# The mixing layer of a decoder trunk in seven products instead of eight, with its sums made by transfers

## The chip, the cores and the metric

The kernel runs on one core of one Trainium2 chip. Its time is device microseconds of one execution: three runs of the kernel before gave 1323.67, 1324.64 and 1323.67 us, median 1323.67. A profile is one further execution; the times of instructions below are from it, counted from the start of its span.

A core has five engines with a queue each: TensorE (PE in the profile, its weight loads PEld), VectorE (DVE), ScalarE (ACT), GpSimd (POOL) and SyncE (SP), which here only issues transfers. TensorE reads SBUF and writes PSUM, which holds eight banks of 128 x 512 floats.

## The reference, cut to what matters

One decoder layer on 1024 tokens of width 1024, in float32. The change lies in the line that makes `x`, and in what hands it on:

```python
merged = jax.nn.sigmoid(g_da) * (y_da @ w_br_da[l]) + jax.nn.sigmoid(g_sw) * (y_sw @ w_br_sw[l])
x = x + merged @ w_mix_out[l]                      # 1024x1024 times 1024x1024
xn = rmsnorm(x, norm_ffn_w[l])
x = x + conv_ffn(xn, w_up[l], conv_w[l], conv_b[l], w_down[l])
```

## The kernel before, in words

Everything lies transposed, channels on the 128 partitions, tokens along the row; "half" is 512 of the 1024 tokens. A float32 product is made of three matmuls: an operand is cut into a high part (ScalarE rounds it, float32r) and a low part (VectorE subtracts), and high x high, high x low and low x high add up in PSUM (`mm3`, L153; `product`, L895). So every weight that is loaded (`load_w`, L132) costs a transfer from SyncE's queue (L129), a ScalarE cast (L139) and a VectorE subtraction (L141), and every operand the same pair (`split`, L820).

The stages, in order of time:

- `project` (L260): the input projections. Most go in pairs through seven products instead of eight (Strassen's scheme in Winograd's form): `sum_pair` (L94) makes four sums of weights on GpSimd, `split_pair` cuts them, `recombine` (L451) puts the seven results together on VectorE.
- `attention` (L492).
- `rest` (L765): for each of eight output chunks m the two branch products, times the gates (GpSimd L791, ScalarE L798, VectorE L802 and L807), summed on GpSimd (L808; the last on VectorE) and cut into high and low parts mh and ml (L811, L812).
- `mix` (L825): the mixing layer. Eight output chunks, each with eight inner chunks x 2 halves x 3 matmuls into two banks. VectorE adds the result to x (L850), ScalarE's queue stores it and scales it, ScalarE squares (L855, L862), GpSimd adds up the squares in `rstd` (L863). After every second chunk `operands` (L874) makes the operands of the next seven products on VectorE.
- `hidden` (L906): the up projection in seven products for each of 22 pairs, then convolution and gate. For j = 0 it first runs three of four inner chunks of five products, then the fourth, then the column sums of squares (L168), which the norm needs. Its weight sums are on GpSimd (L104 to L107). Beside it `sums_of` (L82) makes the weight sums of `down` in DRAM: plain copies on SyncE's queue (L86) and adding transfers on GpSimd's (L87).
- `down` (L1086): the down projection in seven stages, each a product of one weight block and one operand block, added into x.

Order: the program's order gives priorities, and a compile-time scheduler lays each engine's instructions out by them and by when it reckons them ready; on the chip each engine runs its list in order. `next_w` (L65) loads one weight ahead. Raw weights have three buffers (`raw`), high and low parts two each (`wh`, `wl`), so a cast must wait until TensorE is through with the weight two before.

Of the kernel before, what the change touches and what calls it, by code (L numbers as in the profile page):

```python
# [10 lines left out]
F32 = mybir.dt.float32  # L11
F32R = mybir.dt.float32r
AF = mybir.ActivationFunctionType
ALU = mybir.AluOpType
# [30 lines left out]
class Trunk:  # L45
# [18 lines left out]

    def next_w(self, n=2):  # L65

        self.ahead(n)
        return self.wq.pop(0)
# [13 lines left out]
    def sums_of(self):  # L82

        nc, d = self.nc, self.sd
        row = lambda m, r: self.w_dn[m].rearrange("p k c -> p (k c)")[:, r * HK * P:(r + 1) * HK * P]
# [100 lines left out]
    def run(self):  # L186
        nc, tc = self.nc, self.tc
        with ExitStack() as ctx:
# [23 lines left out]
            self.yd = self.dp.tile([8, P, T], F32, name="yd")  # L212
            self.sd = {n: self.dp.tile([4, P, HK * P], F32, name="sd" + n) for n in ("P5", "P6", "P3", "P7")}
            self.wp = ctx.enter_context(tc.tile_pool(name="wp", bufs=2))
            self.qd = self.dp.tile([18, 2, P, T], F32, name="qd")
            self.xctx = ExitStack()
            self.xp = self.xctx.enter_context(tc.tile_pool(name="xp", bufs=1, side="right", reuse_waits="tile"))
# [11 lines left out]
    def plan(self):  # L229
# [16 lines left out]
        self.mix_order = [m for k in range(4) for m in (k, k + 4)]  # L246
        src += [(self.w_mix[m], KC) for m in self.mix_order]
# [12 lines left out]
    def project(self):  # L260
# [4 lines left out]
        self.xl = [self.xp.tile([P, T], F32R, name=f"xl{k}") for k in range(KC)]  # L265
        self.xact = lambda kc, hf: (self.xh[kc][:, hf * H2:(hf + 1) * H2], self.xl[kc][:, hf * H2:(hf + 1) * H2])
        with ExitStack() as ctx:
# [158 lines left out]
            for m in self.plain[3:]:  # L426
# [27 lines left out]
    def recombine(self, ps, us, tp, o, after=None):  # L454
# [11 lines left out]
        with self.tc.issue_after(after) if after is not None else nullcontext():  # L466
            tt(c12, ps["P3"], u4, ALU.add)  # L467
            tt(c21, u3, ps["P4"], ALU.subtract)
# [295 lines left out]
    def rest(self, gctx):  # L764
        nc, tc = self.nc, self.tc  # L765
        with ExitStack() as ctx:
            e = ctx.enter_context
            mctx = ExitStack()
            mh, ml = [], []
            with gctx, ExitStack() as bctx:  # L770
# [13 lines left out]
                mp = mctx.enter_context(tc.tile_pool(name="mp", bufs=1, side="right", reuse_waits="tile"))  # L784
                for m in range(KC):
# [16 lines left out]
                    nc.vector.tensor_tensor(gs[0], gs[0], ps, ALU.mult)  # L802
                    for hf in range(2):
                        ps = self.tl(self.psG, [P, H2], "g")
                        self.mm3(ps, w, yact[1], hf, range(4), o=4)
                        g = gs[1][:, hf * H2:(hf + 1) * H2]
                        nc.vector.tensor_tensor(g, g, ps, ALU.mult)  # L807
                    (nc.vector if m == KC - 1 else nc.gpsimd).tensor_tensor(gs[0], gs[0], gs[1], ALU.add)  # L808
                    a = mp.tile([P, T], F32R, name=f"mh{m}")
                    b = mp.tile([P, T], F32R, name=f"ml{m}")  # L810
                    nc.scalar.copy(a, gs[0])  # L811
# [500 lines left out]
```

## Time and profile before

| what | value |
|---|---|
| median of three runs | 1323.67 us |
| the profiled execution, its own time | 1325.13 us |
| its span in the profile | 1323.3 us |
| mean granted TensorE clock | 0.997 |
| `rest`'s eight chunks on TensorE | about 500.4 to 587.4 us |
| mixing layer on TensorE | 587.4 to 674.5 us |
| `hidden`, first pair until the column sums | 674.5 to 688.1 us |

1.8 us of the execution's time lie outside the span. A row of a timeline has start, length, engine, line, operation, written tile <- read tiles, and in brackets the idle time before it and what ended it. Lengths of neighbours on one engine overlap: the distance between two starts is what an instruction costs in a row, its length what it costs alone.

### The profile page before, as it was taken

To read this page: it belongs to the slowest core of one execution; us is meant where nothing else is said; L and a number is where in the kernel's file an instruction comes from. 1 tells how busy PE (TensorE), PEld (TensorE's weight loads), DVE (VectorE), ACT (ScalarE), POOL (GpSimd) and SP (SyncE) were. 2 spreads that over 40 slices of the span, in tenths; PEclk is the share of its full clock that TensorE was granted. 3 is DMA by queue.
4 is the path that set the end of the run, shared out by engine and by line. 5 is a ranking of instruction groups with operands and counts; after the bars stand their busy time and mean duration, and the time that the engine had idled before them with its cause. 6 is when DMAs were issued, how large, how long until landed. Compare 5 with 4: busy or idle time off the path is not lost.

```text
span 1323.3 us, 17121 instructions
## 1 busy us (share of the span) xinstructions
PE 1310.0 (99%) x6210; PEld 1089.0 (82%) x6210; DVE 1059.7 (80%) x1456; ACT 621.7 (47%) x967; POOL 480.4 (36%) x364
## 2 busy tenths in 40 slices
PE   9999999999999999999999999999999999999997
PEld 7888888888888878888888888888888888878886
DVE  8846775289888976555668999999999999896855
ACT  9432232276667765333444434333343435554543
POOL 0446652000111015651425667666666742000002
PEclk9999999999999999999999999999999999999998
DMA  7334433976554236334333435564536227953434
GB/s 261 126 143 157 145 146 127 266 184 191 143 128 138 84 127 216 139 111 159 128 111 119 177 134 144 147 210 124 167 138 170 77 86 264 323 192 117 161 98 147
DMA packets 71588, 205.96 MB, mean 156 GB/s; under 512 B 8016, under 2 KB 15824, under 8 KB 71376
## 3 DMA queue, kind: packets, MB, share of 16 engines
q1 hardware_dynamic: 57472, 176.03, 39.2%
q0 software_dynamic: 2304, 11.54, 4.6%
q10 hardware_dynamic: 11728, 17.31, 3.6%
q8 instruction: 49, 0.80, 0.2%
q14 instruction: 35, 0.29, 0.1%
HBM read 156.08 MB, written 71.83 MB: 172 GB/s over the span
## 4 chain that ended last, share of the span: by engine, by line
PE 76%; DVE 11%; issue 5%; DMA 4%; POOL 2%; ACT 1%; SPq 0%; POOLq 0%; DVEq 0%; ACTq 0%
PE t L902 27%; PE y L1125 8%; PE d L1125 4%; PE g L160 4%; PE g L161 4%; PE g L162 4%; PE sc L161 3%; PE sc L160 3%; PE sc L162 3%; PE sc L634 3%; DVE c L1071 2%; DVE wl L120 2%; DVE c L1072 2%; PE t L650 1%; DMA rv<-in_w_up 1%
## 5 line engine op out<-in xcount | busy, mean ns | idle before, releaser
L141 DVE TENSOR_TENSOR wl<-raw,wh 128x1024 fp32r<-128x1024 f32 (+2 forms) x85 | 99.7, 1174 | 53.9 <-ACT wh L139 44.0
L139 ACT CAST wh<-raw 128x1024 fp32r<-128x1024 f32 (+2 forms) x85 | 74.1, 873 | 105.8 <-PE y L1125 43.2
L1055 POOL TENSOR_TENSOR us<-us,rstd 128x1024 f32<-128x1024 f32 x42 | 94.8, 2290 | 48.0 <-DVE us L467 31.5
L1069 ACT ACTIVATE c<-us,vecs 128x1024 f32<-128x1024 f32 x44 | 54.8, 1248 | 118.5 <-POOL us L1055 112.9
L120 DVE TENSOR_TENSOR sl<-sf,sh 128x1024 fp32r<-128x1024 f32 x62 | 94.9, 1532 | 14.7 <-ACT sh L118 14.7
L118 ACT CAST sh<-sf 128x1024 fp32r<-128x1024 f32 x62 | 64.7, 1045 | 83.5 <-PE t L902 44.1
L177 POOL TENSOR_TENSOR rs<-ms,mhalf 128x8 f32<-128x8 f32 (+2 forms) x9 | 13.3, 1473 | 234.6 <-DVE ms L175 228.4
L104 POOL TENSOR_TENSOR sf<-rv 128x512 f32<-128x512 f32 x30 | 54.6, 1819 | 116.6 <-DMA rv<-in_w_up 56.4
L1125 PE MATMUL y<-h,wh 128*128 128x512 f32 (+1 forms) x324 | 95.1, 377 | 0.0
L1125 PE MATMUL d<-h,wh 128*128 128x512 f32 x264 | 81.2, 389 | 0.0
L1072 DVE SCALAR_TENSOR_TENSOR c<-us,vecs,c 128x1024 f32<-128x1024 f32 x44 | 75.4, 1746 | 0.1
L160 PE MATMUL g<-xh,wh 128*128 128x512 f32 x176 | 71.0, 403 | 1.5 <-ACT g L563 1.5
L161 PE MATMUL g<-xl,wh 128*128 128x512 f32 x176 | 70.3, 399 | 0.0
L162 PE MATMUL g<-xh,wl 128*128 128x512 f32 x176 | 70.3, 399 | 0.0
L1125 PEld LDWEIGHTS y<-h,wh 128*128 128x128 f32 x324 | 59.4, 188 | 11.0
L106 POOL TENSOR_TENSOR sf<-raw,rv 128x512 f32<-128x512 f32 x30 | 54.9, 1830 | 36.8 <-DVE sl L120 36.8
L1071 DVE SCALAR_TENSOR_TENSOR c<-us,vecs,c 128x1024 f32<-128x1024 f32 x44 | 64.3, 1490 | 1.8 <-ACT c L1069 1.7
L120 DVE TENSOR_TENSOR wl<-raw,wh 128x1024 fp32r<-128x1024 f32 (+1 forms) x32 | 62.8, 1963 | 0.1
L638 DVE CUSTOM_DVE_ANT_0 L<-sc,bias 128x128 f32<-128x128 f32 (+7 forms) x64 | 47.7, 752 | 17.0 <-PE sc L634 13.7
L617 POOL MEMSET aT<- 128x128 f32 x32 | 6.1, 204 | 151.8 <-PE t L663 98.0
L1125 PE MATMUL y<-h,wl 128*128 128x512 f32 (+1 forms) x162 | 61.1, 377 | 0.0
L639 ACT ACTIVATE L<-L,sm 128x128 f32<-128x128 f32 (+7 forms) x64 | 49.6, 778 | 20.0 <-DVE sm L638 17.3
(394 smaller groups left out, 4160.0 us busy)
## 6 DMA issues: line engine op xcount, KB each, us to landing
u<-qd SPq DMA_DIRECT2D x72, 256.0 KB, 6.1
raw<-in_w_up SPq DMA_DIRECT2D x23, 512.0 KB, 4.7
raw<-in_w_in SPq DMA_DIRECT2D x22, 512.0 KB, 3.8
hd<-c SPq DMA_DIRECT2D x22, 512.0 KB, 2.6
sdP<-in_w_down POOLq DMA_DIRECT2D x16, 704.0 KB, 8.3
rv<-in_w_up SPq DMA_DIRECT2D x21, 512.0 KB, 4.6
hc<-hd SPq DMA_DIRECT2D x33, 256.0 KB, 5.4
gr<-gd SPq DMA_DIRECT2D x16, 512.0 KB, 3.4
```

The costliest lines, as they stand in the source:

```text
L118: cast = nc.scalar.copy(hi, src)
L120: low = nc.vector.tensor_tensor(lo, src, hi.bitcast(F32), ALU.subtract)
L139: self.hi = nc.scalar.copy(wh, raw)
L141: self.lo = (eng or nc.vector).tensor_tensor(wl, raw, wh.bitcast(F32), ALU.subtract)
L160: nc.tensor.matmul(ps, wh[:, kc + o, :], ah, start=first and n == 0, stop=False)
L161: nc.tensor.matmul(ps, wh[:, kc + o, :], al, start=False, stop=False)
L162: nc.tensor.matmul(ps, wl[:, kc + o, :], ah, start=False, stop=last and n == len(kcs) - 1)
L902: nc.tensor.matmul(ps, (ah, ah, al)[p][:, k, :], (bh, bl, bh)[p], start=first and n == p == 0, stop=last and p == 2 and n == len(ks) - 1, ...
L1055: i = (nc.vector if m % NF == 0 else nc.gpsimd).tensor_tensor(us[:, 2:], us[:, 2:], self.rstd, ALU.mult)
L1071: nc.vector.scalar_tensor_tensor(c, us[:, 1:T + 1], cw[1], c, ALU.mult, ALU.add)
L1072: nc.vector.scalar_tensor_tensor(c, us[:, 0:T], cw[0], c, ALU.mult, ALU.add)
L1125: nc.tensor.matmul(ps, v[:, k - k0, :], x, start=start and k == i == 0, stop=k == HK - 1 and i == 2, skip_group_check=True)
```

## The change

The mixing layer too goes in seven products: with merged in four blocks (channel halves by token halves) and the weights in four, P1 = A11 B11, P2 = A12 B21, P5 = S1 T1, P6 = S2 T2, P3 = S4 B22, P7 = S3 T3, P4 = A22 T4, where S are sums of weight blocks and T sums of blocks of merged. A stage is one of these: four output chunks x four inner chunks x three matmuls, in two half stages of one weight load each. Every stage is added into x on VectorE as soon as a chunk is done; P6 and P3, P7 and P4 go on in the banks of the stage before them, so that a bank is added in at the points of its running sum.

- The weight sums S are made in DRAM (`sums_of`, now with arguments) while `project` runs its nine pairs: four steps for each pair, 16 copies on SyncE's queue and 16 adding transfers on GpSimd's, 256 KB each.
- The sums T come from 16 adding transfers within SBUF on GpSimd's queue (`add_on`), 256 KB each: four in `rest`, eight after P1, four after P2. For that the gates write some quarters with a minus sign, and merged stays whole (`mr`). Each T is cut when a stage's buffers are free (`split_m`).
- Weights are loaded 14 times instead of 8, all of 512 KB; results are added to x in 28 pieces of 512 columns instead of 8 of 1024.
- Stores of x, squares and the operands for `hidden` go by chunk and half as these become final: in P2 (four), P3, P7 and P4. `finish` and `onward` hold what `mix` and `operands` held.
- `hidden` begins with P1, P5, P3, P7, then P2, whole, then the column sums; the cut of its operands T2 and T4 moves from there into the mixing layer.
- Memory: eight buffers (`slot`) hold in turn the low parts of the input, operands of the mixing layer, of `hidden` and of `down`; x is loaded into eight buffers in the memory of `rest`.

The core of the diff (removed lines of `mix` and `operands` left out, they stand above):

```diff
+    def slot(self, n, shape=[P, 2, H2], dt=F32R):
+        return self.tl(self.ar, shape, f"x{n}", dt)
...
+            sums = self.sums_of(self.md, self.w_mix, H2)
             for j, ms in enumerate(self.pairs):
                 w = self.next_w()
+                for _ in range(4):
+                    with tc.issue_after(self.sync), tc.issue_after(self.sum):
+                        next(sums, None)
...
+                    def gate(g, ps, hf):
+                        if hf == (m < 4):
+                            nc.vector.scalar_tensor_tensor(g, g, -1.0, ps, ALU.mult, ALU.mult)
+                        else:
+                            nc.vector.tensor_tensor(g, g, ps, ALU.mult)
...
+                    (nc.vector if m == KC - 1 else nc.gpsimd).tensor_tensor(mr[:, m], gs[0], gs[1], ALU.add)
+                    for name, hf in ((("B11", 0),) if m < 4 else (("B21", 0), ("B22", 1))):
+                        k = m % 4
+                        t = M[name, k] if name == "B22" else self.slot(m)
+                        M[name, k] = self.split(t[:, 0], t[:, 1], mr[:, m, hf * H2:(hf + 1) * H2])
+                    if m > 3:
+                        self.add_on(mr, m - 4, 0, m - 4, 1)
...
+    def add_on(self, mr, a, ah, b, bh):
+
+        x, y = (mr[:, c, h * H2:(h + 1) * H2] for c, h in ((a, ah), (b, bh)))
+        self.nc.gpsimd.dma_start(x, y, accum_op=ALU.add)
...
+        def finish(m, hf):
+            x = col(m, hf)
+            nc.scalar.dma_start(self.x2d[m, :, hf * H2:(hf + 1) * H2], x)
+            a = acc[:, hf * H2:(hf + 1) * H2]
+            if m == 0:
+                nc.scalar.activation(a, x, AF.Square)
+            else:
+                sq = sqs[:, len(nsq) % 2]
+                nsq.append(m)
+                nc.scalar.activation(sq, x, AF.Square)
+                nc.gpsimd.tensor_tensor(a, a, sq, ALU.add)
+
+        def onward(m, hf):
+            x, k = col(m, hf), m % 4
+            t = t2[k // 2][:, k % 2]
+            if m < 4:
+                nc.scalar.mul(x, x, wcol(m))
+                if hf == 0:
+                    self.B["B11", k] = parts(up["B11", k], x)
+                else:
+                    tt(t, x, col(k, 0), ALU.subtract)
+                    self.B["T1", k] = parts(up["T1", k], t)
+            elif hf:
+                self.B["B22", k] = parts(up["B22", k], x, wcol(m))
+                u = col(k, 1)
+                stt(u, x, wcol(m), u, ALU.mult, ALU.subtract)
+                tt(t, u, col(k, 0), ALU.add)
+                self.B["T3", k] = parts(self.slot(k), u)
+                self.B["T2", k] = parts(up["T2", k], t)
+            else:
+                u = col(m, 1)
+                stt(u, x, wcol(m), t, ALU.mult, ALU.subtract)
+                self.B["T4", k] = parts(up["T4", k], u)
+                self.B["B21", k] = parts(self.slot(4 + k), x, wcol(m))
...
+                for h in range(2):
+                    w = self.next_w()
+                    if n == 0:
+                        for m in (2 * h, 2 * h + 1, 2 * h + 4, 2 * h + 5):
+                            nc.sync.dma_start(xm[m], self.xT[m])
+                    if stage == "P3" and h:
+                        i = [e[1] for e in self.wsrc].index("pair")
+                        pair = self.sum_pair(self.wsrc.pop(i)[0], True)
+                    for m in (2 * h, 2 * h + 1):
+                        ps = chains[which][m]
+                        for k in range(4):
+                            hi, lo = M[b, k]
+                            for i, (v, x) in enumerate(((w[0], hi), (w[0], lo), (w[1], hi))):
+                                nc.tensor.matmul(ps, v[:, m % 2 * 4 + k, :], x, start=start and k == i == 0, stop=k == 3 and i == 2, skip_group_check=True)
+                        x = col(m + o, hf)
+                        tt(x, x, ps, ALU.subtract if o or stage == "P2" else ALU.add)
+                        if done:
+                            finish(m + o, hf)
+                            late.append((m + o, hf))
+                        while len(late) > (m < 3 and o == 0):
+                            onward(*late.pop(0))
+                if stage == "P1":
+                    split_m("T1", 0, 0)
+                    for k in range(4):
+                        self.add_on(mr, k, 1, k + 4, 1)
+                    for k in range(4):
+                        self.add_on(mr, k, 0, k + 4, 1)
+                elif stage == "P2":
+                    split_m("T2", 4, 0, -1.0)
+                    for k in range(4):
+                        self.add_on(mr, k, 0, k + 4, 0)
+                elif stage == "P5":
+                    split_m("T3", 0, 1)
+                elif stage == "P6":
+                    split_m("T4", 4, 0)
...
+        with tc.high_priority(100):
+            return self.split_pair(*pair)
```

More of the change, by code (lines that the diff above doesn't have):

```diff
@@ new lines, in mix @@
+        xm = {m: xmp.tile([P, T], F32, name=f"xm{m}") for m in (4, 5, 6, 7, 3)}
+        x2ctx = ExitStack()
+        xmp2 = x2ctx.enter_context(tc.tile_pool(name="xmp2", bufs=1, reuse_waits="tile"))
+        xm.update((m, xmp2.tile([P, T], F32, name=f"xm{m}")) for m in (2, 1, 0))
+        sqs = self.tl(self.sfp[0], [P, 2, H2], "t42", bufs=1)
+        t2 = [self.tl(self.cpl, [P, 2, H2], "c") for _ in range(2)]
+        acc, nsq, late = self.rstd, [], []
+        col = lambda m, hf: xm[m][:, hf * H2:(hf + 1) * H2]
```

167 lines of the change are left out of this document (74 added, 93 removed).

## The prediction, as put on record

> **What bounds the kernel now.** I read the page's busy shares first, then one line of the chain that ended last, then the groups of TensorE and the busy times by stage.
>
> ```profile
> PE 1310.0 (99%) x6210; PEld 1089.0 (82%) x6210; DVE 1059.7 (80%) x1456; ACT 621.7 (47%) x967; POOL 480.4 (36%) x364
> 64.07 171.36 PE t L902 x756
> L160 PE MATMUL sc<-mh,wh 128*128 128x512 f32 x128 | 49.8, 389 | 0.0
> L161 PE MATMUL sc<-ml,wh 128*128 128x512 f32 x128 | 49.8, 389 | 0.0
> L162 PE MATMUL sc<-mh,wl 128*128 128x512 f32 x128 | 49.8, 389 | 0.0
> ```
>
> TensorE is busy 99% of the span, so only fewer or shorter matmuls, or fewer gaps, make the kernel faster. The length in a group (389 ns) isn't the price of a matmul, for they overlap: 756 of them in a row take 171.36 us, 0.2267 us each. The mixing layer's 3 x 128 = 384 then take 87.0 us.
>
> ```profile
> core 0: us, PE busy (x) PEld busy (x) DVE busy (x) ACT busy (x) POOL busy (x), PEclk, DMA share, GB/s
> 64.00:235.00 171.00, 171.00 (x756) 141.61 (x755) 112.14 (x116) 49.62 (x59) 84.46 (x50) 1.00 0.39 147
> 587.40:674.70 87.30, 87.30 (x386) 72.18 (x385) 52.11 (x47) 33.94 (x44) 24.96 (x17) 1.00 0.40 138
> 674.70:701.80 27.10, 27.10 (x133) 22.82 (x132) 21.16 (x21) 14.32 (x18) 12.36 (x11) 1.00 0.21 81
> 701.80:1106.00 404.20, 404.00 (x1778) 332.71 (x1777) 397.18 (x348) 163.51 (x179) 250.72 (x177) 1.00 0.46 144
> ```
>
> The third row is the mixing layer: TensorE without a gap, VectorE busy for 52 of 87 us. The last row is `hidden`: TensorE full again, VectorE full beside it (397 of 404). So time that TensorE saves in the mixing layer counts to the end only if VectorE, too, comes to `hidden` that much earlier; a backlog there would stay.
>
> **What goes.** Seven stages of 4 x 4 x 3 = 48 matmuls are 336 instead of 384. 48 x 0.2267 = **10.9 us** less on the engine that sets the end. A stage takes 10.9 us, a half stage with its one weight load 5.44.
>
> **What is added where cover is wide.** In `project` the sums in DRAM add 16 copies on SyncE's queue and 16 issues on GpSimd's.
>
> ```profile
> L87 POOL DMA_DIRECT2D sdP<-in_w_down x16: 795/1058/1150, 800.4 to 1012.7; - x16
> DMA to landing us min/median/max: 2.6/5.2/14.5
> raw<-in_w_mix SPq DMA_DIRECT2D x8, 512.0 KB, 3.9
> ```
>
> An issue of the same kind takes GpSimd 1.06 us, 17 us in all; with them it is busy for 101 of 171 us there. An adding transfer waits at the head of GpSimd's queue for its copy, which was issued a pair earlier (84 matmuls, 19 us) and lands in 14.5 us at worst; behind it stand the next pair's four weight sums, for which there is the rest of that pair. I cost it at nothing; if the cover failed, TensorE would wait for a pair's weights, some us at once. The 16 transfers within SBUF are no row of this trace. By the landing of the nearest ones (2.6 to 14.5 us, for 704 KB against 256) the sums stand long before use: T1's are issued in `rest` and used two stages later, T3's and T2's after P1 and used in P7 and P6, 22 us later or more, T4's after P2 for P4. Nothing, then; the upper end is a chain of three landings of 14.5 us against the 22, some 20 us, which I hold for unlikely. Six more weight loads are 3 MB on transfers that are busy for 0.40 of the time: nothing, as long as the casts keep up (below). The eight loads of x now wait for the memory of `rest`'s last gates, free at about 594.7, and land 3.9 us later or more. The first additions into x wait for them, behind these VectorE's next weight part; TensorE needs P1's banks again only in P6, so the list's order decides: 0 to 2 us, taken as 0 because the scheduler can put the weight part first.
>
> **Where a wait is added: P1's second half.** Until now the weight after the first had 10.9 us; now it has 5.44, until 587.4 + 5.44 = 592.8.
>
> ```profile
> 589.84 1.23 DVE L812 TENSOR_TENSOR ml<-gr,mh 128x1024 fp32r<-128x1024 f32 x1 [3.37 <-ACT mh L811]
> 590.98 1.21 DVE L802 TENSOR_TENSOR gr<-gr,sc 128x1024 f32<-128x1024 f32 x1
> 592.11 1.28 DVE L807 TENSOR_TENSOR gr<-gr,g 128x512 f32<-128x512 f32 x2
> 593.43 1.23 DVE L808 TENSOR_TENSOR gr<-gr,gr 128x1024 f32<-128x1024 f32 x1
> 594.57 1.22 DVE L141 TENSOR_TENSOR wl<-raw,wh 128x1024 fp32r<-128x1024 f32 x1
> 595.77 1.22 DVE L812 TENSOR_TENSOR ml<-gr,mh 128x1024 fp32r<-128x1024 f32 x1
> ```
>
> The weight's low part (L141) is done at 595.8, behind the last chunk's gates. Its first reader is the third matmul of the half, at 593.3. As the row stands, TensorE waits 2.5 us. If the compiler puts the part ahead of the sum at 593.43, as it puts it ahead of L812 here, 1.1 us less. I take **+1.4**, bounds 0 and 2.5.
>
> **Where VectorE becomes full: P3, P7, P4.** Prices in a row: an instruction of 512 columns 0.60 us (L807: two in 1.28, one 0.68), a weight part 1.14.
>
> ```profile
> 598.52 1.22 DVE L850 TENSOR_TENSOR x<-x,sc 128x1024 f32<-128x1024 f32 x1 [1.52 <-PE sc L162]
> 599.66 1.22 DVE L141 TENSOR_TENSOR wl<-raw,wh 128x1024 fp32r<-128x1024 f32 x1
> ```
>
> From the start of P3 until the last part of B21:
> - the cut of T4, left from P6: 4 x 0.60 = 2.4
> - P3: two weight parts 2.3, four additions 2.4, T1 of `hidden` (difference and low part, four times) 4.8: 9.5
> - P7: 2.3 + 2.4, and five instructions for each of four chunks (B22, u, t, T3, T2) 12.0: 16.7
> - P4: one weight part 1.1, four additions 2.4, three for each chunk (u, T4, B21) 7.2, and the first pair's four weight parts, which stand early by their priority, 3 x 1.14 + 0.60 = 4.0: 14.7
>
> Together 43.3 us. TensorE, unhindered, asks for the last B21 only in the fifth product of `hidden`: three stages, four products of 2.72 us and nine matmuls later, 32.7 + 10.9 + 2.0 = 45.6. Alone, VectorE would keep up with 2.3 to spare. But it isn't alone.
>
> ```profile
> 612.43 1.29 POOL L863 TENSOR_TENSOR rstd<-rstd,t 128x512 f32<-128x512 f32 x1 [23.70 <-ACT t L862]
> 614.94 1.68 POOL L863 TENSOR_TENSOR rstd<-rstd,t 128x512 f32<-128x512 f32 x1 [1.22 <-ACT t L862]
> 615.40 1.78 DVE L892 TENSOR_TENSOR c<-c,xw 128x512 f32<-128x512 f32 x1
> 603.15 0.69 DVE L888 TENSOR_TENSOR xw<-xw 128x512 f32<-128x512 f32 x1
> L807 DVE TENSOR_TENSOR gr<-gr,g x16: 672/681/689, 510.8 to 592.7; 128x512 f32<-128x512 f32 x16
> 904.59 2.47 DVE L1071 SCALAR_TENSOR_TENSOR c<-us,vecs,c 128x1024 f32<-128x1024 f32 x2
> 906.68 1.53 POOL L104 TENSOR_TENSOR sf<-rv 128x512 f32<-128x512 f32 x1 [3.09 <-DMA rv<-in_w_up]
> 906.98 4.54 DVE L1072 SCALAR_TENSOR_TENSOR c<-us,vecs,c 128x1024 f32<-128x1024 f32 x2
> 908.28 2.16 POOL L105 TENSOR_TENSOR sf<-sf,raw 128x512 f32<-128x512 f32 x1
> 912.74 2.21 POOL L106 TENSOR_TENSOR sf<-raw,rv 128x512 f32<-128x512 f32 x1 [2.26 <-DVE sl L120]
> 914.91 1.30 POOL L107 TENSOR_TENSOR sf<-raw,sf 128x512 f32<-128x512 f32 x1
> ```
>
> L892 takes 1.78 instead of 0.69: it starts inside GpSimd's L863 and ends just after it. L807, which reads PSUM, never takes over 0.69. So of instructions that read two tensors in SBUF, VectorE's wait for GpSimd's, and the other way round. In the stretch above GpSimd has the pair's four sums and ten of the squares (three in P3, four in P7, three of P4's four): 14 x 1.29 = 18.1 us. How much of it falls on VectorE? Bounds: nothing, if it all lies beside additions that read PSUM or waits for TensorE, and the whole 18.1. The nearest rows are the same four sums in `hidden`, where VectorE is full too: they are 4 x 1.29 = 5.2 us, and VectorE lost 2.1 by them (L1072 twice in 4.54, L1071 twice in 2.47), a share of 0.40. 18.1 x 0.40 = 7.3, less the spare 2.3: TensorE waits **5.0 us**. The other end of the range is 18.1 - 2.3 = 15.8.
>
> **The sum:** -10.9 + 1.4 + 5.0 = **-4.5 us**. The profiled execution took 1325.13 us, 1.8 us more than its span; the next would take 1320.6. The median of the runs shown is 1.46 us under it, so the forecast is 1323.67 - 4.5 = **1319.2**. After the column sums the order is as before (two products, two of the next pair), with VectorE less loaded: the cut of T2 and T4 no longer stands there.
>
> **The rivals.**
>
> *VectorE and GpSimd shut each other out for the whole time; slower.* Then VectorE's stretch is 43.3 + 18.1, TensorE waits 15.8, and -10.9 + 1.4 + 15.8 = +6.3, 1330.0 us. It decides from the point where the 18.1 cost more than 11.8 (10.9 - 1.4 + 2.3), a share of 0.65. For it: the lists are fixed at compile time and the chunks' instructions depend on ScalarE's casts in between, so VectorE also has small waits that my 0.60 leaves out. Against it: 0.40 in `hidden`, where the load is as dense. [...] 0.28.
>
> *The cover holds.* GpSimd's work lies beside additions and waits: -10.9 + 1.4 = -9.5, 1314.2 us. For it: L863 and the sums were no hindrance in the mixing layer before, with VectorE at 52 of 87 us. 0.22.
>
> *The weights of P7 and P4 come late.* From P3's second half on, the pair's raw weights hold two of the three buffers, so each load waits for the one before it.
>
> ```profile
> 589.71 1.05 ACT L139 CAST wh<-raw 128x1024 fp32r<-128x1024 f32 x1
> ```
>
> Transfer 3.9, cast 1.05 and low part 1.22 make 6.2 us against a half stage of 5.44, and where VectorE first finishes a chunk (five instructions, 3.0 us), 9.2: 3.7 late, for each of the last two loads 7.5 in all, in place of the 5.0. -10.9 + 1.4 + 7.5 = -2.0, 1321.7 us, no difference that can be told. 0.17.
>
> That the change doesn't do what it says can't be excluded where a scheduler orders the lists: were the sums by transfer late, P6 or P4 would wait with every engine idle. I count it into the first rival.
>
> **How the numbers follow.** The forecast has 0.33. A measurement of this kernel can tell about 0.2%, 2.6 us, from no change. Forecast and cover are faster: 0.55. The late weights lie within: 0.17. The first rival is slower: 0.28. The range goes from the cover without the wait in P1's second half, 1323.67 - 10.9 = 1312.8, to the first rival, 1330.0; outside are shares over the whole lock and late sums. Forecast and cover alone lie between 1312.8 and 1321.
>
> **What would show it.** The mixing layer has 336 matmuls at 0.2267 us. TensorE has a gap of 1 to 2.5 us about 5.4 us after its first, for L141's row. VectorE is nearly without idle time from P3's end until B21, with lengths over 1 us where GpSimd runs, and TensorE's gaps in P4 and the first products of `hidden` sum to some 5 us, waiting for VectorE. The column sums start at about 684 instead of 688.1, and `hidden` runs as long as before. Wrong would be: gaps of 10 us or more there, waits for an adding transfer, or a longer `project` or `hidden`.

## The result, and the profile after

The changed kernel takes 1342.55 us (median of four runs, 1340.74 to 1345.11) against 1323.85 for the kernel before on the same chip: a ratio of 1.0141, 95% interval 1.0121 to 1.0162. It is slower, and outside the range of the prediction (1312.8 to 1330.0). The profiled execution took 1340.74, 15.6 us more than that of before. The experiments ran on other chips of the same kind, where the kernel before took 1325.5 to 1327.2. They are given as ratios to it. The 2 or 3 us between chips are as large as some effects; so beside each ratio stands **T**, from the first matmul of the mixing layer to the first of the column sums in that run's profile. It was 688.1 - 587.4 = 100.7 us before and is 704.35 - 587.66 = 116.7 after; without any hole it would be 89.8 (336 + 60 matmuls of 0.2267). T comes from one execution, whose time lay up to 3.7 us from the median of its runs, so small differences of T say little. One of e10's ten executions took 1865.92 us, at a mean granted clock of 0.65; its ratio leaves it out.

The busy line of the page after, and the busy times by stage. A row has its stretch and length, then TensorE's time, its weight loads', VectorE's, ScalarE's and GpSimd's, each with the count of instructions, then the granted clock, the share of the transfer engines and GB/s:

```profile
PE 1306.0 (98%) x6162; PEld 1084.2 (81%) x6162; DVE 1087.8 (81%) x1518; ACT 634.4 (47%) x1002; POOL 510.3 (38%) x396
```

```profile
core 0: us, PE busy (x) PEld busy (x) DVE busy (x) ACT busy (x) POOL busy (x), PEclk, DMA share, GB/s
64.00:235.00 171.00, 171.00 (x756) 141.57 (x756) 110.98 (x116) 49.44 (x59) 97.56 (x66) 1.00 0.62 190
587.66:609.50 21.84, 21.84 (x97) 17.83 (x95) 13.64 (x18) 7.83 (x11) 5.65 (x6) 1.00 0.89 271
609.50:628.46 18.96, 13.11 (x49) 9.56 (x48) 12.30 (x16) 11.90 (x19) 6.64 (x6) 0.91 0.76 200
628.46:661.74 33.28, 32.52 (x144) 26.57 (x142) 28.35 (x33) 17.28 (x27) 13.25 (x8) 1.00 0.41 136
661.74:690.74 29.00, 17.40 (x53) 12.48 (x52) 28.88 (x35) 16.61 (x26) 11.64 (x6) 0.71 0.41 136
690.74:717.80 27.06, 27.06 (x133) 22.77 (x132) 14.71 (x18) 8.42 (x12) 12.71 (x11) 1.00 0.17 59
717.80:1122.00 404.20, 402.75 (x1775) 332.09 (x1774) 396.25 (x347) 163.13 (x178) 251.42 (x177) 1.00 0.46 143
```

Three rows are as before: `project` takes in 32 more transfers and is full, the first pair of `hidden` is full, and so is the rest. The whole difference lies in the mixing layer, which now lasts from 587.66 to 690.74, 103.1 us, where 336 matmuls of 0.2267 make 76.2. The second row, P1 and P2, has no gap. The third, P5, loses about 8 us, the fourth (P6, P3, most of P7) under 1, the fifth, the last of P7 and P4, about 17, and there the granted clock is 0.71.

TensorE's groups of the mixing layer (count, busy time, mean ns, idle time before) and the rows of its timeline that stand at the holes:

```profile
L953 PE MATMUL m<-x,wh 128*128 128x512 f32 x192 | 63.6, 418 | 15.1 <-ACT wh L142 15.1
L953 PE MATMUL m<-x,wl 128*128 128x512 f32 x96 | 39.4, 418 | 3.1 <-DVE wl L144 3.1
```

```profile
612.99 0.84 PE L953 MATMUL m<-x,wh 128*128 128x512 f32 x2 [3.41 <-ACT wh L142]
...
615.69 0.63 PE L953 MATMUL m<-x,wl 128*128 128x512 f32 x1
616.12 0.98 PE L953 MATMUL m<-x,wh 128*128 128x512 f32 x2
...
617.64 0.39 PE L953 MATMUL m<-x,wl 128*128 128x512 f32 x1
617.86 0.63 PE L953 MATMUL m<-x,wh 128*128 128x512 f32 x2
...
621.81 1.70 PE L953 MATMUL m<-x,wh 128*128 128x512 f32 x6 [1.04 <-ACT wh L142]
```

```profile
667.72 2.07 PE L953 MATMUL m<-x,wh 128*128 128x512 f32 x4 [5.14 <-ACT wh L142]
...
680.79 2.08 PE L953 MATMUL m<-x,wh 128*128 128x512 f32 x4 [5.47 <-ACT wh L142]
683.85 0.79 PE L953 MATMUL m<-x,wl 128*128 128x512 f32 x1 [0.99 <-DVE wl L144]
```

TensorE waits for the high part of a weight in P5 and ahead of both halves of P4, 18.2 us in all with the low parts. That isn't the 26.9 that are lost. The other 8.7 are matmuls behind the holes: from 615.69 to 616.12 one takes 0.43 us, from 617.64 to 617.86 again 0.22. At half speed go some 4 us behind the first two holes, and 8 behind the last.

Why is the weight late in P5? ScalarE's list, and the transfers between 588 and 620 us (by queue: packets, MB, share; by issue: count, KB, us to landing):

```profile
605.27 0.63 ACT L897 ACTIVATE t<-xm 128x512 f32<-128x512 f32 x1 [0.37 <-DVE xm L955]
611.28 0.72 ACT L904 ACTIVATE xm<-xm,vecs 128x512 f32<-128x512 f32 x1 [5.38 <-DMA x2d<-xm]
611.91 1.03 ACT L142 CAST wh<-raw 128x1024 fp32r<-128x1024 f32 x1
```

```profile
q1 hardware_dynamic: 2096, 5.77, 51.1%
q0 software_dynamic: 866, 1.57, 26.7%
...
raw<-mdP SPq DMA_DIRECT2D x4, 512.0 KB, 13.4
mr<-mr POOLq DMA_DIRECT2D x6, 256.0 KB, 7.6
x2d<-xm ACTq DMA_DIRECT2D x4, 256.0 KB, 5.2
```

`onward` scales a chunk of x in place (L904). So it must wait until the store of that chunk (L890, issued just before) has read it, 5.38 us, and the cast of P5's weight stands behind it in ScalarE's list. By the trace that weight had landed at 608.7, before TensorE was through with P2 (609.4): it was the cast that came late, at 611.91. In the kernel before the scaled x went into another tile (`xw`).

Why is it late in P4? ScalarE's, VectorE's and GpSimd's rows, and the busy times from 646 us on:

```profile
666.10 0.62 ACT L881 CAST x<-xm 128x512 fp32r<-128x512 f32 x1 [2.02 <-DVE xm L913]
666.62 1.04 ACT L142 CAST wh<-raw 128x1024 fp32r<-128x1024 f32 x1
...
676.76 1.99 ACT L121 CAST sh<-sf 128x1024 fp32r<-128x1024 f32 x2 [1.61 <-DVE x L882]
...
679.70 1.04 ACT L142 CAST wh<-raw 128x1024 fp32r<-128x1024 f32 x1
```

```profile
651.48 1.78 DVE L882 TENSOR_TENSOR T<-c,T 128x512 fp32r<-128x512 f32 x1
```

```profile
652.67 5.67 POOL L898 TENSOR_TENSOR rstd<-rstd,t 128x512 f32<-128x512 f32 x3
```

```profile
646.00:698.90 52.90, 40.54 (x154) 31.27 (x152) 52.61 (x58) 29.81 (x47) 27.32 (x16) 0.84 0.40 134
```

VectorE is busy for 52.61 of 52.90 us. L882 takes 1.78 where 0.68 is its length alone, and the squares' additions 1.9 instead of 1.29. From 639.5 to 699 VectorE does 65 instructions that would be 44.3 us at 0.60 (two tensors), 0.66 (with a scale) and 1.14 (a weight part); they take 57 without their waits, 12.7 more, beside 15 instructions of GpSimd worth 19.4 at 1.29: a share of 0.66, not 0.40. The prediction counted 14, worth 18.1. And the casts of P4's weights stand in ScalarE's list behind casts of operands that VectorE hasn't made yet.

### The profile page after: what moved, and what is told of

Same layout as the page of the kernel before. It is cut to its first block, busy times and chain, and to the rows that moved or that the text cites. A ratio compares the mean times of both kernels' runs of the same rounds, so it can differ in the third digit from the quotient of the medians.

```text
span 1339.0 us, 17280 instructions
## 1 busy us (share of the span) xinstructions
PE 1306.0 (98%) x6162; PEld 1084.2 (81%) x6162; DVE 1087.8 (81%) x1518; ACT 634.4 (47%) x1002; POOL 510.3 (38%) x396
## 4 chain that ended last, share of the span: by engine, by line
PE 76%; DVE 11%; issue 5%; DMA 3%; ACT 2%; POOL 2%; SPq 0%; POOLq 0%; DVEq 0%; ACTq 0%
PE t L990 29%; PE y L1209 9%; PE d L1209 7%; PE g L163 4%; PE g L164 4%; PE g L165 4%; PE m L953 3%; PE sc L649 3%; DVE c L1155 2%; DVE wl L123 2%; PE t L665 1%; DMA rv<-in_w_up 1%; PE sc L165 1%; PE sc L164 1%; PE sc L163 1%
## 5 line engine op out<-in xcount | busy, mean ns | idle before, releaser
L144 DVE TENSOR_TENSOR wl<-raw,wh 128x1024 fp32r<-128x1024 f32 (+2 forms) x91 | 111.6, 1229 | 47.2 <-ACT wh L142 37.5
L142 ACT CAST wh<-raw 128x1024 fp32r<-128x1024 f32 (+2 forms) x91 | 80.3, 885 | 85.8 <-PE y L1209 44.1
L990 PE MATMUL t<-T,sh 128*128 128x512 f32 x352 | 109.2, 391 | 0.2 <-DVE u L477 0.2
L107 POOL TENSOR_TENSOR sf<-rv 128x512 f32<-128x512 f32 x30 | 56.8, 1894 | 105.2 <-DMA rv<-in_w_up 52.9
L990 PE MATMUL t<-x,wh 128*128 128x512 f32 x248 | 82.2, 389 | 0.0
L953 PE MATMUL m<-x,wh 128*128 128x512 f32 x192 | 63.6, 418 | 15.1 <-ACT wh L142 15.1
L990 PEld LDWEIGHTS t<-T,sh 128*128 128x128 f32 x352 | 65.5, 188 | 15.0 <-DVE u L477 1.6
L164 PE MATMUL g<-x,wh 128*128 128x512 f32 x176 | 70.3, 400 | 0.0
L990 PE MATMUL t<-T,sl 128*128 128x512 f32 x176 | 68.6, 390 | 0.0
L990 PE MATMUL t<-x,sh 128*128 128x512 f32 x212 | 68.2, 389 | 0.0
L1209 PE MATMUL y<-h,wh 128*128 128x512 f32 (+1 forms) x224 | 65.2, 375 | 0.0
```

The lines of the kernel that those rows point to most:

```text
L142: self.hi = nc.scalar.copy(wh, raw)
L144: self.lo = (eng or nc.vector).tensor_tensor(wl, raw, wh.bitcast(F32), ALU.subtract)
L164: nc.tensor.matmul(ps, wh[:, kc + o, :], al, start=False, stop=False)
L953: nc.tensor.matmul(ps, v[:, m % 2 * 4 + k, :], x, start=start and k == i == 0, stop=k == 3 and i == 2, skip_group_check=True)
L990: nc.tensor.matmul(ps, (ah, ah, al)[p][:, k, :], (bh, bl, bh)[p], start=first and n == p == 0, stop=last and p == 2 and n == len(ks) - 1, ...
L1209: nc.tensor.matmul(ps, v[:, k - k0, :], x, start=start and k == i == 0, stop=k == HK - 1 and i == 2, skip_group_check=True)
```

## The experiments

Theory after the result: three things hold TensorE back, (A) the scaling in place behind its store, (B) VectorE full and slowed by GpSimd, with weight casts queued behind its chunks, (C) the slow matmuls behind the holes. The rivals: that the transfers are the root of A, and that the holes only move when one cause, or the slow clock, is taken away. Where a run is said to lose time in P5, that is the time from P2's first matmul to P6's first beyond 21.8 us (96 matmuls); behind P5, from P6's first matmul to the first of the column sums beyond 57.1 (252). The changed kernel loses 8.4 and 18.5. What the prediction and the expectations call the lock or shared ports shows in the traces only as longer instructions where VectorE and GpSimd run beside each other (L882 1.78 us instead of 0.68, an addition of squares 1.9 instead of 1.29); what makes them longer, no run shows. Each experiment is an edit of the changed kernel.

**e1: scale later.** B11 and T1 are scaled while they are cut, and x isn't written in place; its second half is scaled after the last reader.

```diff
-                nc.scalar.mul(x, x, wcol(m))
...
-                    self.B["B11", k] = parts(up["B11", k], x)
+                    self.B["B11", k] = parts(up["B11", k], x, wcol(m))
...
+                with tc.issue_after(self.cut.ins):
+                    nc.scalar.mul(u, u, wcol(k))
```

> The scaling of the new x by the norm's weights no longer stands in place behind the store of x: it is folded into the cut (B11, T1) or done in P7, when the store is long over. Theory 'store wait': TensorE's 8.6 us lost in P5 (P5 takes 19.5 us instead of 10.9) come from ScalarE waiting 5.4 us for the store's transfer, with the cast of P5's weight queued behind; they go, and the kernel takes about 1334 us. Rival 'late transfers': the transfer engines are full from 588 to 610 us and P5's weight itself lands late; then P5 stays over 17 us long and the time over 1340.

Measured: 1.0071 (1.0054 to 1.0088), 0.70% or 9.3 us under the changed kernel by ratio; T 110.3, 6.4 us shorter. P5's holes shrink to two short ones:

```profile
610.43 0.50 PE L954 MATMUL m<-x,wl 128*128 128x512 f32 x1 [0.53 <-DVE wl L144]
619.50 0.50 PE L954 MATMUL m<-x,wl 128*128 128x512 f32 x1 [1.52 <-DVE wl L144]
```

P5 loses 3.2 us instead of 8.4. A holds, at 5 to 9 us: 5 in P5 alone, 6 by T, 9 by ratio.

**e2: no sums of squares.** GpSimd's additions of squares from P3 on are left out, so the norm lacks these chunks.

```diff
-                nc.gpsimd.tensor_tensor(a, a, sq, ALU.add)
+                if hf == 0 and m < 4:
+                    nc.gpsimd.tensor_tensor(a, a, sq, ALU.add)
```

> GpSimd's additions of the squares are left out from P3 on (11 of 14; the norm is then computed from a part of the squares), all else as in the changed kernel. Theory 'shared ports': from P3's start to the last part of B21 VectorE needs 56.9 us for work that takes 44.3 alone, 0.70 of GpSimd's time there; without 11 of 15 GpSimd instructions some 9 us go, the kernel takes about 1333 us. Rival 'order': P4's weights are late because their casts stand deep in ScalarE's list and their transfers wait for one buffer; then the two gaps of 5 us before P4's halves stay and the time is above 1339.

Measured: 1.0068 (1.0045 to 1.0091), 9.7 us under the changed kernel by ratio; T 113.4, 3.3 us shorter. P5's holes stay (3.36 and 2.07), P4's shrink from 5.14 and 5.47 to 2.87 and 4.08. T hides a part: behind P5 6.2 us come back (12.4 lost), while P5 lost 2.8 more. B holds in kind, at 6 to 10 us: instructions that no matmul of this layer waits for cost time.

**e3: matmuls in the holes.** 60 matmuls that nobody reads ahead of P5's first half and P4's halves.

```diff
+                    for _ in range({"P5": (16, 0), "P4": (22, 22)}.get(stage, (0, 0))[h]):
+                        d = M[b, 0][0]
+                        nc.tensor.matmul(chains[0][0], d[:, :P], d, start=True, stop=True, skip_group_check=True)
```

> Matmuls that compute nothing of use are put ahead of P5 (16) and of each half of P4 (22 each), to fill TensorE's gaps there. Theory 'clock': after each gap of 3 to 6 us TensorE runs at half speed for about 4 us (0.43 us a matmul), which costs some 7.7 us in all; with the gaps filled it doesn't slow down, and the kernel takes about 1335 us. Rival 'operands': the slow matmuls have another cause, such as late parts; then they stay, and the time is 1342 or more.

Measured: 1.0097 (1.0079 to 1.0115); T 115.9, 0.8 us shorter, with 13.6 us more matmuls. The last stretch has the full clock, 1.00 instead of 0.71:

```profile
655.00:700.00 45.00, 41.13 (x178) 32.73 (x177) 44.84 (x52) 25.48 (x40) 21.53 (x12) 1.00 0.39 123
```

By the ratio C seemed to hold, 5.8 us of the 8.7; T says that nearly nothing came back. VectorE is full in the same row (44.84 of 45), and TensorE at full speed only arrives earlier at the next wait for it, so in this execution the slow clock didn't set the end there: behind P5 it took 77.7 us with its 44 matmuls more, the changed kernel 75.7. But this execution took 1341.06 us beside e3's median of 1340.20, that of the changed kernel 1340.74 beside 1342.55, so T favours the changed kernel here. What C costs, between nearly nothing and 5.8 us, stays open; e11 tests it again.

**e4: weights first.** The last three weight loads, with their parts, get a priority.

```diff
-                    w = self.next_w()
+                    with tc.high_priority(100 if (stage, h) in (("P7", 0), ("P7", 1), ("P4", 0)) else 0):
+                        w = self.next_w()
```

> The loads of the last three weights (P7's second, both of P4) get a priority 100 instructions earlier, so that casts and low parts stand ahead in the lists of ScalarE and VectorE. Theory 'VectorE is full': the gaps move from P4 to the first products of the up projection, where VectorE's parts are late then; the sum of what TensorE loses in P7, P4 and there stays within 4 us of 18, the time is 1339 to 1344. Rival 'order': the gaps of 5.1 and 5.5 us go, with the slow clock behind them, and the time is about 1328.

Measured: 1.0103 (1.0082 to 1.0123), 1337.5 us by ratio, a little under the expected 1339; T 115.1, 1.6 us shorter. TensorE's idle time in the mixing layer and the first products stays (18.3 us), at other places: 0.22 and 1.35 for P4's weights, but 3.26 and 7.00 for an addition that VectorE does late, the second in `hidden`. As B has it, order alone mostly chooses where TensorE waits.

**e5: e1, and the cuts of T2 and T4 back behind the first five products of `hidden`.** 

> As the first experiment (no scaling in place behind the store), and the cuts of T2 and T4 for the up projection are made behind that stage's first five products, as in the kernel before. That takes 8 of VectorE's instructions, 4.8 us, out of the stretch from P3 to the last part of B21. Theory 'VectorE is full': these 4.8 us and the waits for GpSimd inside them go, and the slow clock after the gaps with them; 5 to 8 us less than the first experiment, a ratio of 1.001 to 1.003. Rival 'order': the gaps come from the place of the casts in ScalarE's list, which this changes little; ratio above 1.005.

```diff
-                self.B["T2", k] = parts(up["T2", k], t)
+                self.cuts.append(("T2", k, up["T2", k], t))
```

Measured: 1.0057 (1.0040 to 1.0074), only 0.14% under e1, T 107.0: a miss. The scheduler put cuts into the stretch all the same (a low part of T at 671.33), and P7's second weight still comes 3.05 us late.

**e6: e5, with the squares summed by adding transfers, and e7: that with the weights first.**

```diff
-                nc.gpsimd.tensor_tensor(a, a, sq, ALU.add)
+                nc.gpsimd.dma_start(a, sq, accum_op=ALU.add)
```

> As e5_cuts_later, and the squares are added up by adding transfers within SBUF from GpSimd's queue instead of GpSimd's own additions (three buffers for the squares instead of two). Theory 'shared ports': VectorE no longer waits for 11 additions of GpSimd in P3, P7 and P4, up to 9 us less as in e2, as far as they are still in TensorE's way: ratio 0.995 to 0.999, faster than before. Rival: the transfers, one behind the other on the same sums, land too late for the column sums, or GpSimd's issues hold VectorE as its additions do; ratio not under that of e5_cuts_later.

> As e6_squares_by_dma, and the last three weight loads with the priority of e4. Theory 'VectorE is full': with its work down, what is left of gaps in P4 is order, 0 to 3 us less than e6_squares_by_dma. Rival: VectorE's parts for the up projection come later by as much; no difference, or 1 to 2 us more.

Measured: 1.0125 (1.0105 to 1.0146), T 116.2, and 1.0078 (1.0063 to 1.0093), T 108.1. A miss for the remedy: the transfers add into one tile, one after the other, 3.3 us each, and squares wait for their buffers ahead of weight casts. In e6 the column sums wait for the last of them (the line of the waits: total, times, longest):

```profile
PE t L171 <- DMA rstd<-t: 6.6, 1, 6.6
```

**e8: e5 with the weights first (e4's edit). e9: that with the twelve additions on VectorE. e10: e8 without them.**

```diff
+                (nc.gpsimd if hf == 0 and m < 4 else nc.vector).tensor_tensor(a, a, sq, ALU.add)
```

> The late scaling, the cuts of T2 and T4 behind the first five products of hidden, and the last three weight loads ahead. If the order of the lists is a cause of its own beside VectorE's load (weights ahead gained 0.4% twice, each time with another part of the order unchanged), it gains that here too: 1.001 to 1.003 of the time before. If VectorE's load alone sets the end and an earlier weight only moves the gap to the chunks, it stays at 1.004 to 1.006.

> As the one before, with the twelve additions of squares from P3 on moved from GpSimd to VectorE. By the theory that GpSimd's additions cost VectorE 0.70 of their 1.29 us each (0.90) and that VectorE does one in 0.60, this is 12 x 0.3 = 3.6 us less, 0.2 to 0.3% under the one before, though VectorE has more to do. If GpSimd's share were the forecast 0.40 (0.52 us each), VectorE's load would grow by 1 us: the same or up to 0.1% more.

> As the first of these three, with the twelve additions left out (the norm's sums of squares then lack these chunks). If the wait for the store, the order and the lock between VectorE and GpSimd are all there is, the saved matmuls come through: 0.994 to 0.996 of the time before, and TensorE's gaps in the mixing layer sum to under 4 us. If VectorE's own work is too much for the stretch even without GpSimd, it stays above 0.998 with gaps of 8 us or more.

Measured: e8 1.0042 (1.0025 to 1.0059), T 105.2, the best version that computes everything; e9 1.0064 (1.0041 to 1.0087), T 110.6; e10 0.9997 (0.9987 to 1.0006), T 98.7. e8 is a miss beside its 1.001 to 1.003 and at its rival's 1.004 to 1.006. In e9 VectorE lost 4 us to GpSimd between 639.5 and 690 instead of 13 in e8, as expected, but had 7.2 us more of its own, and TensorE waits twice for its additions (3.03 and 3.06); no gain, a miss. Its longer T isn't the additions' doing, though: behind P5 it loses 12.0 us, e8 12.7. The rest is P5, with 8.6 lost instead of 2.7: GpSimd's last sum in `rest` begins at 585.1 instead of 580.1, the weight's load 6 us later, it lands at 616.1 instead of 607.8, and its cast waits 4.75 us for it. e10, on the same chip as e8, is half a miss: scaling, order and squares together bring back the 1.4%, not the gain on top. Its busy times:

```profile
649.00:685.00 36.00, 31.68 (x134) 24.46 (x133) 35.00 (x51) 25.95 (x41) 0.10 (x1) 1.00 0.47 168
```

GpSimd is silent and VectorE still full, 35.0 of 36. So VectorE's own work was the next suspect.

**e11: e8 with 28 matmuls in its holes.** The five in P5 overwrite a running sum, which the result then lacks.

```diff
+                    for _ in range({"P5": (0, 5), "P7": (0, 12), "P4": (5, 6)}.get(stage, (0, 0))[h]):
```

> The late scaling, the later cuts and the weights ahead as before (1.004), and 28 matmuls whose result nobody reads ahead of the halves in which TensorE waits (5 in P5, 12 in P7, 11 in P4, 6.3 us in all), so that it isn't idle there. If the slow matmuls after a gap (5 us beyond the gaps themselves) are what a gap costs twice, 3 to 5 us come back: 1.0005 to 1.002. If VectorE, which then is full all the same, sets the end, TensorE only waits a little longer at the next place: 1.003 to 1.005.

Measured: 1.0060 (1.0037 to 1.0083); T 110.3, 5.1 us longer than e8's. Behind P5 it takes 71.8 us with 23 of the 28, e8 takes 69.9. No gain, as e3's T had it; but the five in P5 must also wait until VectorE has read that bank, and P5's weight came 3.3 us later than in e8, so that this run alone would not decide.

**e12: e10 with less work for VectorE**, the low parts of 20 operands of `hidden` left out.

```diff
+                if not low:
+                    return hi, hi
                 tt(lo, src, hi.bitcast(F32), ALU.subtract)
```

> As the run with all known causes out (0.9997, VectorE without idle time from 649 to 685 us), and in addition the low parts of the operands B11, T1, B22, T3 and B21 of hidden left out, the high parts standing in for them: 20 instructions, 16 of them in P3, P7 and P4, some 10.5 us of VectorE's work (this and the squares are left out of the result). If VectorE's own work was what still held the saved matmuls back, they now come through: 0.992 to 0.995, TensorE's gaps in the mixing layer under 3 us in all. If it is the order of ScalarE's casts or the transfers, the gaps stay and so does the time: 0.998 to 1.000.

Measured: 0.9973 (0.9955 to 0.9990), T 96.4; faster than the kernel before, less than expected. Its busy times from P6 to the first products:

```profile
639.50:684.50 45.00, 44.48 (x195) 36.13 (x194) 36.02 (x48) 31.86 (x50) 7.41 (x5) 1.00 0.53 176
```

VectorE has 9 us to spare and TensorE is full. That settles P7 and P4: behind P5 e12 loses 1.1 us, where e10 lost 5.9. Of the 6.6 us that its T still loses, 4.6 lie in P5, where the weight's cast waits 3.24 us for its transfer, `raw<-mdP`, issued late as in e9.

**e13: x by halves, and e14, e15: that in e8 and in e12.** Each half of x is loaded a stage ahead of its use.

```diff
-                    if n == 0:
-                        for m in (2 * h, 2 * h + 1, 2 * h + 4, 2 * h + 5):
-                            nc.sync.dma_start(xm[m], self.xT[m])
+                    if n < 4:
+                        for m in (2 * h + (0, 4, 0, 4)[n], 2 * h + 1 + (0, 4, 0, 4)[n]):
+                            q = slice((0, 1, 1, 0)[n] * H2, ((0, 1, 1, 0)[n] + 1) * H2)
+                            nc.sync.dma_start(xm[m][:, q], self.xT[m][:, q])
```

> The changed kernel with one edit: x loaded by halves, each a stage before its first use, instead of whole in P1 (same bytes, 1 MB in each of P1, P2, P5, P6). If the crowd of transfers between 583 and 610 us is the root of P5's gap (the store that the scaling waits for landed in 5 to 6 us there, the weight of P5 in over 9), both land earlier and P5 loses 4 to 8 us less: 1.008 to 1.011. If any store is too slow for an in-place scaling right behind it, whatever the load: 1.012 to 1.014.

> Late scaling, later cuts and weights ahead (1.004) with x by halves. If the transfers' load still costs something in P5 (a gap of 1.5 us and slow matmuls behind it, in some runs a weight that lands 2.5 us late), 2 to 3 us come back: 1.002 to 1.003. If P5's rest is VectorE's low part of the weight alone: 1.004 as before.

> The run with VectorE's load lightened (0.9973; additions of squares and 20 low parts left out) with x by halves. Its loss was nearly all in P5, 6 us, behind a weight that landed late. If that is the transfers' load, it comes through: 0.992 to 0.995. If not: 0.997 to 0.998.

Measured: 1.0134 (1.0118 to 1.0149), 1.0068 (1.0050 to 1.0087) and 0.9997 (0.9987 to 1.0006), T 118.4, 111.7 and 99.3. No gain, and a loss in the latter two. The edit didn't do what it was meant to do: 8.41 MB moved between 588 and 620 us, as without it, halves of 256 KB landed no sooner (7.6 us) than whole chunks (7.8), and squares now waited for x.

**e16: without the twelve adding transfers after P1 and P2** (T2, T3 and T4 then lack a term). **e17: those of T3 and T4 one stage later; e18: that in e8.**

```diff
-                    for k in range(4):
-                        self.add_on(mr, k, 1, k + 4, 1)
...
-                    for k in range(4):
-                        self.add_on(mr, k, 0, k + 4, 1)
...
-                    for k in range(4):
-                        self.add_on(mr, k, 0, k + 4, 0)
```

> The changed kernel without the twelve adding transfers within SBUF after P1 and P2 (T2, T3 and T4 then lack a term; the four of T1 stay). x by halves had left as many bytes in flight between 588 and 620 us (8.4 MB), so it had not taken the load away; this does, by 3 MB written. If the crowd of transfers is the root of P5's loss (8.5 us), most of it comes back: 1.007 to 1.010, with the weight of P5 landing in under 6 us instead of 13. If the scaling that waits for its store is enough by itself: 1.012 to 1.014.

> The changed kernel with all sums made, but those of T3 issued after P2 and those of T4 after P5, one stage later than before. If the crowd is the root, a third to a half of P5's loss comes back: 1.010 to 1.012. If not, or if the crowd only moves into P5: 1.013 to 1.015.

> Late scaling, later cuts, weights ahead (1.0042) and the sums of T3 and T4 one stage later. If P5's rest there (a gap of 1.5 us, slow matmuls behind it) is the crowd's: 1.002 to 1.003. If it is VectorE's low part of the weight: 1.004.

Measured: e16 1.0086 (1.0071 to 1.0101), T 112.6; e17 1.0130 (1.0113 to 1.0146), T 117.1; e18 1.0052 (1.0037 to 1.0067), T 108.9. The transfers and ScalarE's list of e16:

```profile
raw<-mdP SPq DMA_DIRECT2D x5, 512.0 KB, 5.1
x2d<-xm ACTq DMA_DIRECT2D x4, 256.0 KB, 3.0
```

```profile
607.59 0.72 ACT L904 ACTIVATE xm<-xm,vecs 128x512 f32<-128x512 f32 x1 [1.36 <-DMA x2d<-xm]
608.21 1.03 ACT L142 CAST wh<-raw 128x1024 fp32r<-128x1024 f32 x1
```

Without these twelve a weight lands in 5.1 us instead of 13.4 (medians), a store in 3.0 instead of 5.2, the scaling waits 1.36 instead of 5.38, and 4 us (T) to 7 us (ratio) come back. So the crowd of transfers is one root of P5's loss, and the adds within SBUF are a large part of the crowd; the scaling in place hands it to TensorE. Neither alone is all of it: P5 loses 8.4 us, 4.8 without the twelve adds, 3.2 with the late scaling; a run with both was not made. And e16 also takes twelve issues from GpSimd and lets T be cut earlier, which it can't tell apart. To move them a stage later doesn't help (e17, e18): the transfer engines are full from 594 to 612 us all the same (a share of 1.05 and 1.04).

Side by side, the time lost in P5 and behind it:

| kernel | P5, us | behind P5, us |
|---|---|---|
| changed | 8.4 | 18.5 |
| e2: no squares | 11.2 | 12.4 |
| e16: no adds | 4.8 | 18.0 |
| e1: late scaling | 3.2 | 17.3 |
| e5: and later cuts | 3.4 | 13.9 |
| e8: and weights first | 2.7 | 12.7 |
| e9: e8, squares on VectorE | 8.6 | 12.0 |
| e10: e8, no squares | 3.0 | 5.9 |
| e12: e10, less work on VectorE | 4.6 | 1.1 |

Scaling and transfers act on P5. What lies behind P5 goes step by step with VectorE's load: its own cuts, GpSimd's squares, the low parts.

## Why the prediction was wrong, point by point

- **-10.9 for 48 matmuls: right.** 336 remain, and where weights are there they run as priced: P1 and P2 are 97 in 21.84 us. `project` with its 32 transfers is unchanged, too.
- **+1.4 for L141's row in P1's second half: 0.** The compiler put the part (here L144) ahead of P1's cut, and TensorE has no gap there:

```profile
588.58 1.22 DVE L831 TENSOR_TENSOR mr<-gr,gr 128x1024 f32<-128x1024 f32 x1
589.72 1.22 DVE L144 TENSOR_TENSOR wl<-raw,wh 128x1024 fp32r<-128x1024 f32 x1
```

- **The adds within SBUF at nothing: the first step that failed.** I asked only whether the sums come in time. They do. But they were priced by their landing time alone, and not by what they take from the transfers beside them, with x and four weights in the same 32 us: "transfers that are busy for 0.40 of the time" is a mean over the layer; from 594 to 612 they are full (a share of 1.04). e16 prices the twelve at 4 to 7 us.
- **The scaling, for which the sum has no term: the second.** I didn't ask what a moved instruction waits for when it begins to write in place. 5 to 9 us by e1, in part the same microseconds as the step above, not in addition.
- **+5.0 where VectorE is full: right in place, mis-sized, and the largest miss.** TensorE lost 18.5 us from P6's first matmul to the column sums. The 43.3 us of work are 44.3 by the trace, and the stretch is full as said. The share 0.40 was wrong: VectorE lost 0.85 us for each of GpSimd's instructions, and 0.87 to 0.89 in e1, e4 and e8, a share of 0.66 to 0.69. By my own sum that alone makes 12.7 - 2.3 = 10.4 instead of 5.0; without the squares 6 to 7 us came back (e2, e10). The "spare 2.3" wasn't there either: with the squares gone, VectorE is still full (e10), and only with 20 instructions fewer does TensorE run through (e12).
- **What no step held:** the casts of weights behind casts of operands in ScalarE's list, which turn VectorE's lateness into whole holes, and the half speed behind the holes (0.43 us a matmul). The latter is 8.7 of the 26.9 us in the accounts; how much of it is a cause stays open. In e3's profile TensorE at full speed waited instead.
- **The rivals.** The first had the right sign, and VectorE and GpSimd did hold each other up: L882 took 1.78 us beside GpSimd instead of 0.68. Its point of decision, a share of 0.65, was just reached (0.66); at 1330.0 it was still 12.5 us short, mostly by P5, which it didn't hold. That VectorE loses the whole of GpSimd's time was its assumption, and the runs don't show it: it lost two thirds, 0.85 us of each 1.29. The late weights (the third rival) came, through ScalarE's list rather than through raw buffers.

The sum as it was: -10.9 + 8 (P5) + 17 and 1 (the rest of the layer) is +15 or so, where the profiles differ by 15.6. What stays open: the sizes, which ratio and T give up to 6 us apart; the cost of the slow clock; the rest of P5's loss once the scaling is late, which goes with the time at which its weight lands (607.8 in e8, 611.1 in e11, 613.8 in e12, 616.1 in e9); and I found no version that computes everything and beats the kernel before.

## What to carry to other kernels

A product saved on a full engine is worth what the engines that feed it can spare in just that stretch: sum their work there, and add what they lose to each other; here each GpSimd addition took two thirds of its length from a full VectorE, 0.85 of 1.29 us. Ask of every operation that is moved what it now waits for (here a write in place waited 5.38 us for the store that reads the tile) and what stands behind it in its engine's list. Price transfers by the crowd in their own stretch, not by a mean over the stage: here a weight landed in 13.4 us, and in 5.1 without twelve of the transfers beside it.

## What the runs showed of the hardware

- **Half speed behind a hole.** After holes of 3.41, 5.14 and 5.47 us, matmuls of 0.22 us took 0.43; the granted clock is 0.50 from 613.5 to 616.9, from 664.7 to 671.4 and from 678.4 to 688.5, in part while TensorE is still idle. The full clock was back 3.9 and 3.8 us after work began again, and 7.8 where a hole of 0.99 stands in between. The length of the hole alone doesn't decide. In e16 a hole of 2.32 us was enough, and in e18 holes of 1.62 and 0.52 close together (slow matmuls from 614.29 to 617.70, a mean clock of 0.72 from 612 to 618). After 1.04 us in the changed kernel (621.81, six in 1.70), 2.45 in e12 (615.00, a mean clock of 1.00 from 609.31 to 628.17) and 3.03 in e18 (656.94, then 0.22 to 0.24 us a matmul from 657.28 to 661.83) the matmuls weren't slower. What decides, the runs don't show. The row of e16's hole, and two behind it that are 0.43 apart for one matmul:

```profile
618.18 2.07 PE L953 MATMUL m<-x,wh 128*128 128x512 f32 x6 [2.32 <-ACT wh L142]
620.04 0.63 PE L953 MATMUL m<-x,wl 128*128 128x512 f32 x1
620.47 1.05 PE L953 MATMUL m<-x,wh 128*128 128x512 f32 x2
```

That the clock slows doesn't yet mean that it costs: e3 had it at 1.00 from 655 to 700, and T all but the same.

- **Adds within SBUF took more time for a MB.** Between 588 and 620 us the queue of the adding transfers moved 1.57 MB and took 26.7% of the transfer engines' time, SyncE's plain queue 5.77 MB and 51.1%: 17.0% for a MB against 8.9%, 1.9 times as much. The plain queue took 8.4% for a MB in e16, without the twelve adds.
- **What GpSimd costs VectorE was no fixed share.** It took 0.85 to 0.89 us of VectorE for each 1.29 us of GpSimd where VectorE was full (the changed kernel, e1, e4, e8), about 0.4 for each of the pair's four sums in e12, where VectorE had 9 us to spare, and 0.52 in `hidden` before, though VectorE was full there. So a share is to be taken from a stretch of the same make.
